# Merging three gated branches: the additions of the second and third branch as accumulating DMA transfers

## The chip, the cores and the metric

The kernel runs on one core of one Trainium2 chip. The metric is the device time in microseconds (us) of one execution; three executions of the kernel before were timed. The profile is one more execution, recorded by the hardware profiler; its times are counted from the start of its span, which runs from the first to the last instruction.

## What is computed

One layer of a decoder trunk on 256 tokens of width 2048, in float32. A normalised input goes through one wide projection; three mixers (a linear attention "GLA", a sparse attention "NSA" and a state-space mixer "SSD") each give an output of width 1024. Each is projected to 2048, multiplied by a sigmoid gate, and the three are added. The merged sum goes through an output projection, and a feed-forward network follows.

```python
gate = jax.nn.sigmoid(m_g).reshape(bsz, T, N_BRANCH, D)
merged = (gate[:, :, 0] * (y_gla @ w_branch[l, 0])
          + gate[:, :, 1] * (y_nsa @ w_branch[l, 1])
          + gate[:, :, 2] * (y_ssm @ w_branch[l, 2]))
x = x + rms_norm(merged @ w_out[l], norm_post_mix[l])
h = rms_norm(x, norm_pre_ffn[l])
f = (jax.nn.silu(h @ w_ffn_gate[l]) * (h @ w_ffn_up[l])) @ w_ffn_down[l]
```

## The kernel before, in words

All large products are streamed. The weights come from HBM in chunks of 512 KB (tile `raw`, four buffers), loaded by DMAs on the queue of SyncE (SP, line 75). Each chunk is split into two parts that the matrix engine multiplies at reduced precision: ScalarE (ACT) makes the high part `hi` (line 84), VectorE (DVE) the rest `lo` (line 87). There are three buffers of each. TensorE (PE) then multiplies a chunk in twelve matmuls of 128x512 (line 78): two blocks of 128 rows, two tiles of 128 tokens (t = 0 and t = 1), three products each. The activations are stationary; one product of 256 tokens by 512 features is `gemm_a`. In the last chunk of a `gemm_a` the token tiles go one after the other, so that t = 0 is ready earlier than t = 1.

The merge is `branch(b, ...)`. It is called for the SSD mixer first (it starts the sum), then for GLA, then for NSA (the last). In each call four groups of 512 features (j = 0 to 3) are worked on. For each j, a `gemm_a` of the input projection gives the gate, which ScalarE turns into `sg` by a sigmoid; then a `gemm_a` with `w_branch` gives the branch's product in PSUM, tile `g`. For each token tile, `ev` multiplies `sg` by `g` on VectorE (line 952); in the first branch the result is the sum `mg[j]` itself, in the other two it is written over `sg` and added to `mg[j]` by a second VectorE instruction (line 954). `mg[j]` of each token tile has 128 partitions of 512 floats, 256 KB.

In the last branch, when t = 1 is done, `to_fl` transposes the finished `mg[j]` on TensorE with eight small matmuls (tile `tr`, line 81), and ScalarE and VectorE split the result into `mh` and `ml`, the stationary operands of the output projection. The first of the two token tiles needs two of the eight transposes before the others, as the scheduler has placed them.

`sg` and `mg`, like most activations, sit in 32 buffers of one pool (`slot`), which are used again when their last reader is done. Work of the mixers that is not yet finished is woven in between the chunks: during the GLA branch it is the second half of the NSA mixer; during the last branch nothing is woven in. A scheduler places all instructions on the engines' queues ahead of time by its own cost estimates; each engine then takes its queue strictly in order. GpSimd (POOL) does a few set-up instructions at the start and one addition at the very end (line 1087).

Of the kernel before, what the change touches and what calls it, by code (L numbers as in the profile page):

```python
# [12 lines left out]
ALU = mybir.AluOpType  # L13
# [17 lines left out]
def trunk_kernel(ctx: ExitStack, tc: tile.TileContext, x, w_in, gla_a2, gla_a_bias, gla_norm,  # L31
# [36 lines left out]
    pinned = [False]  # L68

    def pin(ins):  # L70
        """In the pinned parts the engines keep the order in which the work is written down."""
        return tc.keep_in_program_order(ins) if pinned[0] else ins

    def dma(out, in_):
# [28 lines left out]
            kw["accum_out"] = acc  # L103
        return pin(S.activation(out=o, in_=a, func=f, scale=scale, **kw))  # L104

# [1 line left out]
    ident = const([P, P], name="ident")  # L107
    make_identity(nc, ident)
    eps = const([P, 1], name="eps")
# [1 line left out]
    one1 = const([P, 1], name="one1")  # L111
    V.memset(one1, 1.0)

    # parameters along the features, as columns
    cols, pcol = {}, {}

    def load_cols(key, parts):
# [50 lines left out]
        tt(lo, src, hi.bitcast(F32), ALU.subtract)  # L168

    def to_fl(src, hi, lo, i, gain=None):  # L170
        """Two feature tiles of src(k, t) = [tokens of tile t, features of tile k], transposed, scaled by
        their gains and split into hi and lo, as tiles 2i and 2i + 1 of the slot."""
        pt = pm("tr")
        for k in range(2):
            for t in range(2):
                tr(pt[:, k * T + t * P:k * T + (t + 1) * P], src(2 * i + k, t), ident)
        if gain is None:
            split(pt.rearrange("p (a n) -> p a n", a=2), hi[:, 2 * i:2 * i + 2, :], lo[:, 2 * i:2 * i + 2, :])
        else:
            for k in range(2):  # L180
                act(hi[:, 2 * i + k, :], pt[:, k * T:(k + 1) * T], AF.Copy, scale=gain(2 * i + k))
            for k in range(2):
                stt(lo[:, 2 * i + k, :], pt[:, k * T:(k + 1) * T], gain(2 * i + k), hi[:, 2 * i + k, :].bitcast(F32),
                    ALU.mult, ALU.subtract)
# [2 lines left out]
        act(o, a, AF.Sqrt, bias=eps[:, :], scale=1.0 / w)  # L187
        V.reciprocal(out=o, in_=o)

# [1 line left out]
    bg, started, first, raws = [], [], [], []  # L191

    def pump(n):
# [20 lines left out]
        while bg and (gen is None or any(b[0] is gen for b in bg)):  # L214
            pump(1)

# [1 line left out]
    def wchunk(fill, c, width):  # L218
        """The split goes ahead of the woven work; the loads too, once the activations are in."""
        if not started:  # L220
            return first.pop(0) if first else wchunk_(fill, c, width)
        with tc.high_priority(W_AHEAD):
            return wchunk_(fill, c, width)
# [19 lines left out]
        return fill  # L243

    def gemm_b(fill, width, xh, xl, KT, evac):
        """out[features, tokens]: the weights are stationary."""
        nt = width // P
        kc = 1024 // width
        g = [ps.tile([P, 2, T], F32, tag="g", bufs=4, name=nm("g")) for _ in range((nt + 1) // 2)]
        for c in range(KT // kc):  # L250
            hi, lo = wchunk(fill, c, width)
            for a in range(kc):
                k = c * kc + a
                for n in range(nt):
                    wh = hi[:, a * width + n * P:a * width + (n + 1) * P]
                    wl = lo[:, a * width + n * P:a * width + (n + 1) * P]
                    mm(g[n // 2][:, n % 2, :], wh, xh(k), k == 0 and n % 2 == 0, False)
                    mm(g[n // 2][:, n % 2, :], wh, xl(k), False, False)
                    mm(g[n // 2][:, n % 2, :], wl, xh(k), False, k == KT - 1)
            if c == KT // kc - 1:  # L260
                evac(g)
            tick()

    def gemm_a(fill, xh, xl, KT, evac, first=1, last=1):
        """out[tokens, 512 features]: the activations are stationary. The first and the last chunks go one
        token tile after the other, so that the tiles' beginnings and ends lie apart."""
        g = [ps.tile([P, 512], F32, tag="g", bufs=4, name=nm("g")) for _ in range(2)]
        n = KT // 2
        groups = [list(range(first))] + [[c] for c in range(first, n - last)] + [list(range(n - last, n))]
        for cs in groups:  # L270
            ws = [wchunk(fill, c, 512) for c in cs]
            ks = [(2 * c + a, hi[:, a * 512:(a + 1) * 512], lo[:, a * 512:(a + 1) * 512])
                  for c, (hi, lo) in zip(cs, ws) for a in range(2)]
            for t in range(2):
                for k, wh, wl in ks:
                    mm(g[t], xh(k)[:, t * P:(t + 1) * P], wh, k == 0, False)
                    mm(g[t], xh(k)[:, t * P:(t + 1) * P], wl, False, False)
                    mm(g[t], xl(k)[:, t * P:(t + 1) * P], wh, False, k == KT - 1)
                if cs[-1] == n - 1:
                    evac(g[t], t)  # L280
            for _ in cs:
                tick()

# [1 line left out]
    xt, hh, hl = [], [], []  # L285
    rsT = const([P, 2], name="rsT")
    rB = const([P, T], name="rB")
# [8 lines left out]
    first_fill = filler(w_in[0], C_SX, 512)  # L296

    def load_first():
        """The activations and the weights they meet first, the very first in small pieces."""
        pinned[0] = True  # L300
        for j in range(4):
            xt.append(slot(name="x"))
# [55 lines left out]
    def in_a(c0, evac):  # L358
        gemm_a(filler(w_in[0], c0, 512), hT, lT, 16, evac)

# [1 line left out]
    load_first()  # L362
    later(first_norm(), [1, 1, 1, 0, 1, 2, 2])
    conv = []
# [17 lines left out]
    for j in range(4):  # L382
        in_b(C_SX + 512 * j, 512, conv_evac(j))

# [1 line left out]
    sm = const([P, T], name="sm")  # L386

    def small_fill(c, raw):
# [6 lines left out]

    gemm_b(small_fill, 128, hT, lT, 16, lambda g: tt(sm, g[0][:, 0, :], rB, ALU.mult))

# [1 line left out]
    mneg = const([P, P], name="mneg")  # L399
    G.memset(mneg, 0.0)  # L400
    G.affine_select(out=mneg, in_=mneg, pattern=[[1, P]], compare_op=ALU.is_ge, fill=-1e30, base=0,
# [106 lines left out]
            ys_l.append(lo)  # L508

    def both(f):  # L510
        """An evacuation of both token tiles at the second one's end, for one table load."""
        gs = []

        def e(g, t):
            gs.append(g)
            if t == 1:
                f(gs[0], 0)
                pinned[0] = True
                f(gs[1], 1)
                pinned[0] = False  # L520
                gs.clear()
        return e
# [5 lines left out]
            act(halves(o[-1])[:, t, :], g, AF.Silu, scale=rsT[:, t:t + 1])  # L528
        return both(f)

# [1 line left out]
    eb, ei = [], []  # L532
    ebc = const([P, 8, 4], name="ebc")

    def decay():
        a2t = flat(slot(name="a2"))[:16, :]
        dma(out=a2t, in_=gla_a2[0])
        # one pass carries the products of the hi and lo parts, which lie one below the other
        a2s, sms = flat(slot(F32R, "a2s")), temp(F32R, "sms")[:, :T]
        for m, f in ((a2s, a2t), (sms, sm[:16, :])):  # L540
            V.memset(m[:96, :].bitcast(F32), 0.0)
# [134 lines left out]
            yg_h.append(hi)  # L676
            yg_l.append(lo)

# [1 line left out]
    nq, kv = [], []  # L680

    def nq_evac(g):
        """Queries, and for float32r: hi over lo of the even heads, lo over hi of the odd ones."""
        qf, L, QA, QB = slot(name="qf"), slot(F32R, "ql"), slot(F32R, "qa"), slot(F32R, "qb")
        for b in range(2):
            stt(qf[:, 2 * b:2 * b + 2, :], g[b], 0.125, rB2, ALU.mult, ALU.mult)
        for q_, H in ((slice(0, 64), QA), (slice(64, 128), QB)):
            S.copy(out=H[q_], in_=qf[q_])
            tt(L[q_], qf[q_], H[q_].bitcast(F32), ALU.subtract)
        dma(out=QA[64:128].bitcast(F32), in_=L[0:64].bitcast(F32))  # L690
        dma(out=QB[0:64].bitcast(F32), in_=L[64:128].bitcast(F32))
        nq.append((qf, QA, QB))
# [114 lines left out]
    def nsa(g):  # L807
# [30 lines left out]
                  pcm[:, 2:4, t * P:(t + 1) * P])  # L838
            yield

        # a pair of heads at a time; both full attentions and the compressed one add up in one accumulator,
        # the values' hi parts in its upper half and their lo parts in its lower half
        yt = slot(name="yn")
        hi, lo = slot(F32R, "ynh"), slot(F32R, "ynl")
        for f in range(4):
# [64 lines left out]
        yn_h.append(hi)  # L910
        yn_l.append(lo)

# [1 line left out]
    g_ssd, g_decay, g_gla, g_keys = ssd(), decay(), gla(), nsa_keys()  # L914
    finish()
    later(g_ssd, R_SSD)
# [17 lines left out]
    g_nsa = nsa(0)  # L934
    later(g_nsa, R_NSA)

# [1 line left out]
    mg = [None] * 4  # L938
    mh, ml = [], []

    def branch(b, yh, yl, first, last):
        for j in range(4):
# [5 lines left out]
            def ev(g, t):  # L948
                if first and t == 0:
                    mg[j] = slot(name="mg")  # L950
                sgt, mgt = halves(sg)[:, t, :], halves(mg[j])[:, t, :]
                tt(mgt if first else sgt, sgt, g, ALU.mult)
                if not first:
                    tt(mgt, mgt, sgt, ALU.add)
                if last and t == 1:
                    mh.append(slot(F32R, "mh"))
                    ml.append(slot(F32R, "ml"))
                    for i in range(2):
                        to_fl(lambda k, t: halves(mg[j])[:, t, k * P:(k + 1) * P], mh[j], ml[j], i)
# [11 lines left out]
    finish(g_nsa)  # L971
    branch(1, yn_h, yn_l, False, True)

# [1 line left out]
    gB = [slot(name="gB") for _ in range(2)]  # L975
    for h in range(2):
        dma(out=flat(gB[h]), in_=norm_post_mix[0, h * 1024:(h + 1) * 1024].partition_broadcast(P))
# [66 lines left out]
        for t in range(2):  # L1044
            token_rs(rs2, xss, t)

# [1 line left out]
    g_n2 = second_norm()  # L1048
    later(g_n2, 1.0)
    fh, fl = [], []  # L1050
# [67 lines left out]
```

## Time and profile before

| | |
|---|---|
| time, median of three executions | 1746.62 us (1746.36 to 1747.38) |
| span of the profiled execution | 1744.4 us (what lies around the span, against the median: 2.2 us) |
| TensorE busy | 1726.8 us, 99% of the span |
| VectorE busy | 1018.4 us, 58% |
| ScalarE busy | 857.3 us, 49% |
| GpSimd busy | 5.5 us |
| DMA, one hardware queue | 322.82 MB, 62.5% of 16 engines' span |
| the GLA and the NSA branch | about 622 to 778 us, and 778 to 916 us |

Only the span stands in the profile; the time of the profiled execution as a whole is not recorded, so the median of the three timed ones stands for it. A matmul's recorded duration overlaps the next one's (they are pipelined); the distance between their starts tells the rate. In the rows, PEld is the load of a stationary operand, which waits on behalf of the matmul that follows it. SPq is SyncE's own queue: a row there is the issue of a DMA, not its transfer.

### The profile page before, as it was taken

How to read it: one execution, taken by the hardware profiler on the slowest of the kernel's cores; microseconds unless marked ns; L12 is line 12 of the kernel's file. 1: busy time of each engine (PE TensorE's matmuls, PEld its weight loads, DVE VectorE, ACT ScalarE, POOL GpSimd, SP SyncE). 2: the span in 40 equal slices, each digit the busy share in tenths (PEclk: the TensorE clock that was granted, in tenths of full speed). 3: DMA queues.
4: the chain of work that ended last, by engine and by line, in shares of the span. 5: the costliest groups of instructions: out<-in, count | busy, mean ns of one | idle time of the engine just before them, and what ended most of it. 6: DMA issues, size and time to landing. Idle time of an engine off the chain costs nothing.

```text
span 1744.4 us, 22985 instructions
## 1 busy us (share of the span) xinstructions
PE 1726.8 (99%) x8951; PEld 1463.6 (84%) x8951; DVE 1018.4 (58%) x1366; ACT 857.3 (49%) x1129; POOL 5.5 (0%) x37
## 2 busy tenths in 40 slices
PE   8999999999999999999999999999999999999998
PEld 8998889999887887788888778888888888888886
DVE  5687667565766666765555564544544545544444
ACT  6556467343656556554444464444444444443443
POOL 0000000000000000000000000000000000000000
PEclk9999999999999999999999999999999999999999
DMA  7666655755555565556667676666666666766664
GB/s 234 183 175 194 178 170 171 215 146 156 171 157 159 167 182 157 157 158 191 190 185 251 194 221 189 192 184 190 191 185 190 190 186 191 225 205 195 205 205 147
DMA packets 178497, 324.28 MB, mean 186 GB/s; under 512 B 21010, under 2 KB 24772, under 8 KB 178388
## 3 DMA queue, kind: packets, MB, share of 16 engines
q1 hardware_dynamic: 178388, 322.82, 62.5%
q8 instruction: 70, 1.15, 0.3%
q14 instruction: 39, 0.32, 0.1%
HBM read 316.47 MB, written 4.21 MB: 184 GB/s over the span
## 4 chain that ended last, share of the span: by engine, by line
PE 96%; DVE 1%; ACT 1%; DMA 1%; issue 1%; SPq 0%; DVEq 0%; ACTq 0%
PE g L78 89%; PE tr L81 1%; PE po L78 1%; PE ps L78 1%; DMA raw<-in_w_in_dram 1%; DVE lo L87 1%; PE p L81 1%; PE py L78 1%; PE pa L78 1%; PE m L81 0%; ACT x L104 0%; ACT hi L84 0%; DVE ab L576 0%; PE ph L78 0%; DMA x<-in_x_dram 0%
## 5 line engine op out<-in xcount | busy, mean ns | idle before, releaser
L87 DVE TENSOR_TENSOR lo<-raw,hi 128x1024 fp32r<-128x1024 f32 (+1 forms) x583 | 712.3, 1222 | 654.7 <-ACT hi L84 653.5
L84 ACT CAST hi<-raw 128x1024 fp32r<-128x1024 f32 (+1 forms) x583 | 611.9, 1050 | 802.4 <-PE g L78 765.7
L78 PE MATMUL g<-lo,fh 128*128 128x512 f32 x1056 | 412.2, 390 | 1.4 <-DVE lo L87 1.4
L78 PE MATMUL g<-hi,fl 128*128 128x512 f32 x1056 | 412.1, 390 | 0.0
L78 PE MATMUL g<-hi,fh 128*128 128x512 f32 x1056 | 411.3, 390 | 0.0
L78 PEld LDWEIGHTS g<-lo,fh 128*128 128x128 f32 x1056 | 198.3, 188 | 42.7 <-DVE lo L87 1.9
L78 PEld LDWEIGHTS g<-hi,fl 128*128 128x128 f32 x1056 | 198.4, 188 | 40.7 <-DVE fl L96 0.4
L78 PEld LDWEIGHTS g<-hi,fh 128*128 128x128 f32 x1056 | 198.3, 188 | 40.7 <-ACT fh L104 0.2
L78 PE MATMUL g<-hi,hh 128*128 128x512 f32 x576 | 229.9, 399 | 0.0
L78 PE MATMUL g<-lo,hh 128*128 128x512 f32 x576 | 226.1, 392 | 0.0
L78 PE MATMUL g<-hi,hl 128*128 128x512 f32 x576 | 225.8, 392 | 0.0
L78 PE MATMUL g<-hh,hi 128*128 128x256 f32 x752 | 215.6, 287 | 0.0
L78 PE MATMUL g<-hh,lo 128*128 128x256 f32 x752 | 213.6, 285 | 1.5 <-DVE lo L87 1.5
L78 PE MATMUL g<-hl,hi 128*128 128x256 f32 x752 | 213.2, 284 | 0.0
L78 PEld LDWEIGHTS g<-hh,lo 128*128 128x128 f32 x752 | 144.5, 192 | 2.6 <-DVE lo L87 2.5
L78 PEld LDWEIGHTS g<-hh,hi 128*128 128x128 f32 x752 | 144.8, 193 | 0.4
L78 PEld LDWEIGHTS g<-hl,hi 128*128 128x128 f32 x752 | 144.9, 193 | 0.1
L78 PEld LDWEIGHTS g<-hi,hh 128*128 128x128 f32 x576 | 108.4, 188 | 23.2 <-ACT hi L84 0.7
L78 PEld LDWEIGHTS g<-hi,hl 128*128 128x128 f32 x576 | 108.2, 188 | 22.5
L78 PEld LDWEIGHTS g<-lo,hh 128*128 128x128 f32 x576 | 108.4, 188 | 20.3
L104 ACT ACT_TABLE_LOAD x43 | 55.2, 1283 | 4.0 <-DVE ab L576 2.5
L78 PE MATMUL g<-hi,ml 128*128 128x512 f32 x128 | 50.1, 391 | 0.0
(275 smaller groups left out, 1337.6 us busy)
## 6 DMA issues: line engine op xcount, KB each, us to landing
raw<-in_w_in_dram SPq DMA_DIRECT2D x235, 512.0 KB, 3.6
raw<-in_w_ffn_gate_dram SPq DMA_DIRECT2D x88, 512.0 KB, 3.7
raw<-in_w_ffn_up_dram SPq DMA_DIRECT2D x88, 512.0 KB, 3.7
raw<-in_w_ffn_down_dram SPq DMA_DIRECT2D x88, 512.0 KB, 4.6
raw<-in_w_branch_dram SPq DMA_DIRECT2D x48, 512.0 KB, 3.8
raw<-in_w_out_dram SPq DMA_DIRECT2D x32, 512.0 KB, 4.3
x<-in_x_dram SPq DMA_DIRECT2D x7, 512.0 KB, 6.0
cumB<-scr SPq DMA_DIRECT2D x4, 512.0 KB, 5.5
```

Of the source, the lines that this page charges most:

```text
L78: PE.matmul(o, lhsT=l, rhs=r, start=start, stop=stop, skip_group_check=True)
L81: pin(PE.transpose(o, a, i))
L84: pin(S.copy(out=o, in_=a))
L87: pin(V.tensor_tensor(out=o, in0=a, in1=b, op=op))
L104: return pin(S.activation(out=o, in_=a, func=f, scale=scale, **kw))
```

## The change

Line 954 is replaced. The product of the second and third branch is still made on VectorE; the addition to `mg[j]` is a DMA, issued from GpSimd's queue, that reads `sg` and accumulates it onto `mg[j]`, both in SBUF. There are 16 such DMAs of 256 KB: two branches, four groups, two token tiles. The rest of the text's difference is comments and docstrings that were taken out.

```diff
                 sgt, mgt = halves(sg)[:, t, :], halves(mg[j])[:, t, :]
                 tt(mgt if first else sgt, sgt, g, ALU.mult)
                 if not first:
-                    tt(mgt, mgt, sgt, ALU.add)
+                    G.dma_start(out=mgt, in_=sgt, accum_op=ALU.add)
                 if last and t == 1:
```

On TensorE, at the end of the last branch's last group (j = 3). `mg_5935` is the merged sum of this group, `tr_8470` and `tr_8477` the PSUM tiles of its transposes; `g_8496` and `g_8497` are the two token tiles of the next product (the output projection's first), whose first chunk is `hi_8500`, `lo_8501` and the second `hi_8518`, `lo_8519`. Of the kernel before, from the seventh matmul of that first chunk on:

```order
L78 MATMUL g_8497<-hi_8500,mh_7739 128x512
L78 MATMUL g_8497<-lo_8501,mh_7739 128x512
L81 MATMUL tr_8470<-ident_72,mg_5935 128x128 [waits DVE_49,PE_49]
L81 MATMUL tr_8477<-ident_72,mg_5935 128x128 [waits PE_49]
L78 MATMUL g_8497<-hi_8500,ml_7740 128x512
L78 MATMUL g_8497<-hi_8500,mh_7739 128x512
L78 MATMUL g_8497<-lo_8501,mh_7739 128x512
L78 MATMUL g_8497<-hi_8500,ml_7740 128x512
L78 MATMUL g_8496<-hi_8518,mh_7739 128x512 [waits Activation_49]
L78 MATMUL g_8496<-lo_8519,mh_7739 128x512
L81 MATMUL tr_8470<-ident_72,mg_5935 128x128 [waits DVE_49]
L81 MATMUL tr_8470<-ident_72,mg_5935 128x128 x2
```

Of the changed kernel, from the last matmul of the first chunk on:

```order
L78 MATMUL g_8497<-hi_8500,ml_7740 128x512
L78 MATMUL g_8496<-hi_8518,mh_7739 128x512 [waits Activation_49]
L78 MATMUL g_8496<-lo_8519,mh_7739 128x512 [waits DVE_49]
L81 MATMUL tr_8470<-ident_72,mg_5935 128x128 [waits DMASW6_49,PE_49]
L81 MATMUL tr_8477<-ident_72,mg_5935 128x128 [waits PE_49]
L78 MATMUL g_8496<-hi_8518,ml_7740 128x512
L78 MATMUL g_8496<-hi_8518,mh_7739 128x512
L81 MATMUL tr_8470<-ident_72,mg_5935 128x128 [waits DMASW7_49]
L81 MATMUL tr_8470<-ident_72,mg_5935 128x128 x2
L81 MATMUL tr_8477<-ident_72,mg_5935 128x128 x3
L78 MATMUL g_8496<-lo_8519,mh_7739 128x512
```

The transposes of t = 0 stood behind eight matmuls of the next product and waited for VectorE; now they stand behind fourteen and wait for a DMA from GpSimd (DMASW6). Those of t = 1 stood behind fourteen matmuls and stand behind sixteen (DMASW7). The other three groups of the last branch read the same.

On GpSimd's queue, the last rows of the program, of the changed kernel (of these, the kernel before has the one of line 1087):

```order
L954 DMA mg_5613<-sg_7998 128x512 [waits DMASW4_49,DVE_49]
L954 DMA mg_5613<-sg_7998 128x512 [waits DMASW5_49,DVE_49]
L954 DMA mg_5935<-sg_8241 128x512 [waits DMASW6_49,DVE_49]
L954 DMA mg_5935<-sg_8241 128x512 [waits DMASW7_49,DVE_49]
L1087 TENSOR_TENSOR x_2154_12694<-no_13901,x_2154_12694 128x512 [waits DMAHW0_49,PE_49,Activation_49]
```

Each DMA waits for its product on VectorE and for the same group's DMA of the branch before; nothing else stands between them on this queue.

On SyncE's queue, a little later: `x_1373` is the input for the residual, loaded into the buffer that `sg_8241` leaves. Before:

```order
L75 DMA raw_8652<-in_w_out_dram 128x2x512 [waits DMAHW5_49,DVE_49]
L75 DMA raw_8670<-in_w_out_dram 128x2x512 [waits DMAHW6_49,DVE_49]
L75 DMA x_1373_8488<-in_x_dram 128x2x512
L75 DMA raw_8688<-in_w_out_dram 128x2x512 [waits DMAHW7_49,DVE_49]
L75 DMA raw_8706<-in_w_out_dram 128x2x512 [waits DMAHW1_49,DVE_49]
```

After:

```order
L75 DMA raw_8652<-in_w_out_dram 128x2x512 [waits DMAHW5_49,DVE_49]
L75 DMA x_1373_8488<-in_x_dram 128x2x512 [waits DMASW7_49,DMASW6_49]
L75 DMA raw_8670<-in_w_out_dram 128x2x512 [waits DMAHW6_49,DVE_49]
L75 DMA raw_8688<-in_w_out_dram 128x2x512 [waits DMAHW7_49,DVE_49]
L75 DMA raw_8706<-in_w_out_dram 128x2x512 [waits DMAHW1_49,DVE_49]
```

The load of `x_1373` moved ahead of one weight load and waits for the last two accumulations.

In the first two groups of the GLA branch the scheduler also moved the woven NSA work: VectorE's scalings of `sw` come earlier by the additions that are gone, and the transposes of `sw` on TensorE some ten matmuls earlier.

## Rows read from the trace of the kernel before

**Rows 1.** The page: busy time by engine, and the chain that ended last

```profile
PE 1726.8 (99%) x8951; PEld 1463.6 (84%) x8951; DVE 1018.4 (58%) x1366; ACT 857.3 (49%) x1129; POOL 5.5 (0%) x37
...
PE 96%; DVE 1%; ACT 1%; DMA 1%; issue 1%; SPq 0%; DVEq 0%; ACTq 0%
```

**Rows 2.** Stretches: busy us (instructions) by engine, granted clock, DMA share, GB/s

```profile
650.00:800.00 150.00, 149.99 (x679) 119.22 (x678) 100.30 (x156) 85.15 (x142) 0.00 (x0) 1.00 0.55 161
800.00:920.00 120.00, 120.00 (x546) 98.96 (x545) 66.16 (x67) 55.01 (x60) 0.00 (x0) 1.00 0.65 192
911.00:918.00 7.00, 7.00 (x36) 5.72 (x35) 6.08 (x9) 4.22 (x5) 0.00 (x0) 1.00 0.70 211
```

**Rows 3.** Waits from 800 to 930 us: us in total, times, longest

```profile
ACT hi L84 <- PE g L78: 70.5, 46, 1.9
DVE lo L87 <- ACT hi L84: 58.6, 42, 1.5
...
PEld tr L81 <- DVE mg L87: 0.9, 4, 0.2
```

**Rows 4.** Tile mg: its additions, ns min/median/max, first and last start

```profile
L87 DVE TENSOR_TENSOR mg<-mg,sg x16: 639/684/692, 657.9 to 914.3; 128x512 f32<-128x512 f32 x16
```

**Rows 5.** Waits of PEld from 640 to 800 us (most of it the GLA branch)

```profile
PEld ps L78 <- issue: 5.3, 20, 0.4
...
PEld po L78 <- ACT w L84: 0.5, 2, 0.3
...
PEld p L81 <- DVE sw L91: 0.4, 2, 0.2
```

**Rows 6.** Timeline, end of the last group: start, us, engine, line, instruction

```profile
911.36 1.28 DVE L87 TENSOR_TENSOR sg<-sg,g 128x512 f32<-128x512 f32 x2
...
911.47 3.30 SPq L75 DMA_DIRECT2D raw<-in_w_out_dram  x2
911.65 0.39 PE L78 MATMUL g<-hi,mh 128*128 128x512 f32 x1
...
912.56 0.68 DVE L87 TENSOR_TENSOR mg<-mg,sg 128x512 f32<-128x512 f32 x1
...
913.16 1.22 DVE L87 TENSOR_TENSOR lo<-raw,hi 128x1024 fp32r<-128x1024 f32 x1
```

**Rows 7.** The chain from 800 to 920 us: start, us, piece

```profile
882.30 31.33 PE g L78 x138
913.63 0.22 PE tr L81 x2
```

**Rows 8.** DMA issues: engine, count, KB each, median us to landing

```profile
raw<-in_w_out_dram SPq DMA_DIRECT2D x32, 512.0 KB, 4.3
...
x1d<-x SPq DMA_DIRECT2D x4, 512.0 KB, 6.1
...
out_dram<-x SPq DMA_DIRECT2D x8, 256.0 KB, 2.4
...
qa<-ql SPq DMA_DIRECT2D x2, 256.0 KB, 4.3
```

**Rows 9.** Timeline of SyncE's queue about 440 us and about 920 us

```profile
439.59 0.37 SPq L75 DMA_DIRECT2D raw<-in_w_in_dram  x1
440.79 0.47 SPq L75 DMA_DIRECT2D qa<-ql  x1
...
920.59 3.08 SPq L75 DMA_DIRECT2D raw<-in_w_out_dram  x2
923.72 0.47 SPq L75 DMA_DIRECT2D x<-in_x_dram  x1
```

## The prediction

> **What bounds the kernel now.** I read the page first: TensorE is busy for 99% of the span and makes up 96% of the chain that ended last [rows 1]. So a microsecond of another engine is worth something only where TensorE waits for it. The stretches that hold the two changed branches say the same more sharply: TensorE is busy for 149.99 of 150 us and for all of 120 us, at the full granted clock (1.00, the 2.4 GHz level), while VectorE works 100 of 150 and 66 of 120 us [rows 2]. The waits give the direction: ScalarE's splits wait for TensorE (70.5 us), VectorE's for ScalarE (58.6 us) [rows 3]; weights are there early and everyone waits for the matmuls. What the sum's additions cost TensorE today is one row: four waits of the transposes for `mg`, 0.9 us in all, all in the last branch [rows 3].
>
> **What is removed.** 16 additions of 0.684 us on VectorE, 10.9 us of its 1018 [rows 1, 4]. Almost none of that is on the path. In the last branch it is at most the 0.9 us of waits. In the GLA branch nobody waits for `mg`, but the woven NSA work shares VectorE; the waits there that VectorE's or ScalarE's being late could explain are 0.4 and 0.5 us, in two pieces each, while the largest row of TensorE's waits has no engine behind it [rows 5]. The reordered `sw` work in two groups arrives earlier on both engines by about the same amount; I put it at 0, with 1 us either way over both groups (about the sum of those two rows).
>
> **What is added, and where it lies.** In the GLA branch the eight transfers have no reader until the same group of the next branch, more than 100 us later; they cost nothing on the path. In the last branch TensorE itself stands before the transposes, and everything behind them on its queue waits too. So the price is set at four places, one per group, and the question is one time: from the end of a product on VectorE to the landing of its transfer.
>
> How much of it is covered, at j = 3. The two products run on VectorE from 911.36 to 912.64, 0.68 us each with a small overlap; so t = 0 ends at about 912.04 and t = 1 at 912.64 [rows 6]. The next product's first matmul starts at 911.65 [rows 6]. Matmuls follow at 31.33/138 = 0.227 us [rows 7]. The transposes of t = 0 now stand behind fourteen of them: 911.65 + 14 x 0.227 = 914.83. Then two transposes (0.22 [rows 7]) and two matmuls (0.45): 915.50 for t = 1. So both transfers have about 2.8 us (914.83 - 912.04 = 2.79, 915.50 - 912.64 = 2.86) before TensorE stops.
>
> How long a transfer takes. No transfer of the kernel before is issued by GpSimd, and none accumulates, so this is a bound from both sides. The lower end is 2.4 us: 256 KB from SBUF to HBM at the end of the kernel, with no weights beside it [rows 8]. The nearest row is `qa<-ql`: 256 KB within SBUF, issued 1.2 us behind a weight load as the accumulation will be 0.6 to 1.2 us behind one (911.47): 4.3 us [rows 6, 8, 9]. An accumulation moves more than a copy, since it reads the sum as well as the product; twice the bytes beside weight loads is `x1d<-x`, 512 KB, 6.1 us [rows 8]. I take the middle of 4.3 and 6.1, **5.2 us**. The descriptors, which GpSimd makes, the second transfer behind the first, and an addition that must read before it writes have no row; a whole further round trip for them (2.4 us) on top of 6.1 gives the upper end, 8.5 us.
>
> The wait at one place: 912.04 + 5.2 - 914.83 = 2.4 us for t = 0; t = 1 then lands at 917.84, and TensorE gets to it at 915.50 + 2.4 = 917.9, with no further wait. Four places: 9.6 us. None of it comes back: TensorE has no idle time later in which to catch up, and the work that piles up meanwhile (splits of the next weights) was waiting for TensorE already [rows 3].
>
> What else is queued behind these waits. ScalarE's and VectorE's splits of the transposes (`mh`, `ml`) come later, with the split of a weight chunk behind them on each queue; TensorE has one chunk under way and two more split by then, about 2 x 12 x 0.227 = 5.4 us of work, which covers a split (1.22 us on VectorE [rows 6]). `mh` of the last group is needed in the seventh chunk of the output projection, six chunks or 16 us on. On SyncE, the load of `x_1373` now waits for the last transfers, with a weight load behind it. It is reached after `raw_8652`, at 920.59 + 0.37 = 920.96 [rows 9], 8.3 us after the last product, so a transfer of 5.2 us has landed; and the weight load behind it was not free to go before some 923.3 (it and the one before fill 920.59 to 923.67 [rows 9]). Cost nothing; it would begin to cost past some 10 us.
>
> **The sum.** Against the profiled execution, 1744.4 us of span: 4 x 2.4 = +9.6, the waits for VectorE's addition -0.9, the woven work 0: 1753.1 us. The median of the timed runs is 2.2 us above this span: **1755.3 us**, 0.5% slower.
>
> **The rivals.** *The transfer is hidden.* It lands in at most 2.8 us, TensorE never waits, and 0.9 us of waits go: 1744.4 - 0.9 + 2.2 = 1745.7 us. For it speaks the 2.4 us row [rows 8], against it that this row has the DMA engines to itself, while here weight loads take 0.70 of them [rows 2]. It decides at the landing: with up to 3.95 us (a wait of 1.16 at each place, 4.6 - 0.9 = 3.7 us in all) the time stays within 0.2% of before, so this is the case that ends not slower. The Trainium skill speaks for it: "DMA: Bandwidth & Descriptors", section on the anatomy of one DMA on the GpSimd path, has a fit of about 2.0 us plus the bytes at 436 GB/s, by which an estimate for 256 KB is 2.6 us and the sum would be 1745.7 us; no run here shows a transfer on that path yet, and the row for 256 KB within SBUF is 4.3 us from another queue.
>
> *GpSimd is held up by VectorE.* Straight behind the second product VectorE runs a split of 1.22 us, `lo<-raw,hi` [rows 6] (it moves up to about 912.6, since the addition is gone). If GpSimd could not make descriptors while VectorE works in SBUF, each transfer would start up to 1.2 us later: 4 x (2.4 + 1.2) - 0.9 = +13.5, 1760 us. Nothing in the trace bears on it, as GpSimd is idle there [rows 2].
>
> *VectorE's relief is worth more than its waits.* For a gain of over 3.5 us the transfers would have to be hidden and the woven work of the GLA branch speed up by over 2.6 us; its waits on VectorE and ScalarE are below 1 us [rows 5].
>
> **How the numbers follow.** The forecast, landings between 3.95 and 8.5 us: 0.68. Held up by VectorE: 0.08. Hidden or nearly: 0.22. The gain: 0.02. Differences within 0.2% (3.5 us) are about what a measurement of this kernel can tell from no change; so faster 0.02, same 0.22, slower 0.68 + 0.08 = 0.76. The ends of the unknown: hidden, with 1 us of luck, 1744.7; the upper end, 912.04 + 8.5 - 914.83 = 5.7 us at four places, 22.8 - 0.9 + 1 = +22.9, 1769.5 us. For 8 in 10 I cut a part at either end: 1747 to 1767.
>
> **What would show it.** Right: TensorE's weight loads for `tr` wait about 2.4 us for the DMA `mg<-sg` at four places (t = 0), near 814, 850, 886 and 922 us, and hardly at t = 1; the transfers land 5.2 us after issue; VectorE's busy time falls by 11 us; SyncE's `x` load waits for none. Wrong: landings under 3 us with no such wait (hidden), landings that follow VectorE's splits (held up), a wait at t = 1 as long as at t = 0 (the two transfers go one after the other), or a change outside the four places: in the woven part from 650 to 800 us, or in the weight loads' landing.

## The result, and the profile after

The changed kernel takes 1765.58 us (median of four runs, 1765.24 to 1768.27) against 1746.86 us for the kernel before (four runs): the ratio is 1.011, 95% interval 1.0097 to 1.0122. It is slower, by 18.7 us where 8.7 was forecast. The profiled execution has a span of 1764.1 us, 19.7 more than before. It is one of the four; TensorE's granted clock, averaged over the span, was 0.994 to 0.996 in them (0.995 in the profiled one), so how much of the work ran at the lower clock differs a little from one to the next.

The page of the changed kernel, busy time and the chain that ended last, answering [rows 1]:

```profile
span 1764.1 us, 23020 instructions
...
PE 1733.7 (98%) x8951; PEld 1468.0 (83%) x8951; DVE 1010.3 (57%) x1350; ACT 858.7 (49%) x1129; POOL 19.6 (1%) x53
...
PE 88%; issue 7%; DMA 2%; DVE 2%; ACT 1%; POOL 0%; SPq 0%; DVEq 0%; POOLq 0%; ACTq 0%
```

VectorE has its sixteen instructions less and GpSimd its sixteen more. TensorE, with the same 8951 matmuls, is busy for 6.9 us longer, and it also stands for longer: 19.7 - 6.9 leaves 12.8 us of new idle time. So there are two losses, and the forecast had only one kind.

The idle time is in the waits from 640 to 960 us of the changed kernel, which holds both branches (engine and line, what it waited for: us in total, times, longest). It answers the last row of [rows 3], where these transposes waited 0.9 us for VectorE:

```profile
PE tr L81 <- DMA mg<-sg: 11.6, 8, 1.9
PEld tr L81 <- issue: 8.3, 4, 2.3
...
PEld tr L81 <- DMA mg<-sg: 6.7, 4, 1.7
```

TensorE waited for the transfers eight times, at all four groups of the last branch, once for each token tile; the PEld rows are the same stops seen by the load of the stationary operand. The waits of the woven work in the GLA branch [rows 5] stand as they were (its largest row is 5.3 us before and after).

The first of the four places, in the timeline of the changed kernel (start, us, engine, line, instruction; in brackets the idle time before it and what ended it), answering [rows 6]:

```profile
810.96 1.28 DVE L87 TENSOR_TENSOR sg<-sg,g 128x512 f32<-128x512 f32 x2
...
811.94 1.75 POOL L954 DMA_DIRECT2D mg<-sg  x2 [31.77 <-DVE sg L87]
...
814.20 0.39 PE L78 MATMUL g<-lo,hh 128*128 128x512 f32 x1
...
816.25 0.41 PE L81 MATMUL tr<-ident,mg 128*128 128x128 f32 x2 [1.66 <-DMA mg<-sg]
...
816.73 0.40 PE L78 MATMUL g<-hi,hh 128*128 128x512 f32 x1
818.38 1.19 PE L81 MATMUL tr<-ident,mg 128*128 128x128 f32 x6 [1.26 <-DMA mg<-sg]
...
819.80 0.63 PE L78 MATMUL g<-hi,hl 128*128 128x512 f32 x1
...
820.23 0.63 PE L78 MATMUL g<-hi,hh 128*128 128x512 f32 x1
```

The first product ends at about 811.64 and its transfer has landed by 816.2, 4.6 us later; the second ends at 812.24 and its transfer has landed by 818.35, 6.1 us later. TensorE stops for 1.66 us, does two transposes and two matmuls, and stops for another 1.26 us. Then the matmuls, 0.39 us long and 0.227 apart until then, are 0.63 us long and 0.43 apart. The stretches of the changed kernel around it, and two later ones (columns as in [rows 2]), say why:

```profile
811.00:814.40 3.40, 3.40 (x16) 2.63 (x14) 2.47 (x4) 1.28 (x2) 1.75 (x2) 1.00 0.75 210
814.40:818.40 4.00, 1.08 (x6) 0.49 (x5) 1.23 (x1) 0.82 (x1) 0.00 (x0) 1.00 1.05 202
818.40:822.40 4.00, 4.00 (x14) 3.37 (x15) 1.33 (x2) 1.18 (x2) 0.00 (x0) 0.57 0.45 173
822.40:826.00 3.60, 3.60 (x18) 2.98 (x17) 1.23 (x1) 1.61 (x2) 0.00 (x0) 1.00 0.00 0
895.00:899.00 4.00, 4.00 (x21) 3.41 (x22) 1.52 (x3) 2.13 (x3) 0.00 (x0) 1.00 0.47 177
932.60:936.60 4.00, 4.00 (x17) 3.39 (x16) 1.33 (x2) 3.16 (x5) 0.00 (x0) 0.72 0.93 338
1024.00:1027.00 3.00, 3.00 (x14) 2.48 (x13) 2.55 (x8) 1.95 (x8) 0.00 (x0) 0.50 0.92 270
```

TensorE is busy for only 1.08 of the 4 us in which it stops twice, at a granted clock of 1.00, and behind the stops the clock is 0.57 over 4 us: most of it is granted at the lower level, 1.2 GHz. At 822.4 it is back at 2.4 GHz; in finer slices the lower level lasts from about 818.7 to 822.2, 3.5 us. The same is seen behind the second and the fourth place (3.1 and 3.5 us), not behind the third (895 to 899: 1.00), and once more in the norm that follows the output projection (1024 to 1027: 0.50), where the kernel before has 1.00 for the same work.

The norm's lower clock is not shown to come from the change. One of the kernels below has the merge of the kernel before and only adds three transfers behind the end of the program; its norm has the lower clock too (the first row is of the kernel before, the second of that kernel):

```profile
1006.00:1009.00 3.00, 3.00 (x21) 2.39 (x19) 3.00 (x8) 2.95 (x11) 0.00 (x0) 1.00 1.02 337
...
1006.60:1009.60 3.00, 3.00 (x13) 2.35 (x12) 2.79 (x8) 2.17 (x9) 0.00 (x0) 0.50 0.96 331
```

**Where the 19.7 us are.** Each place begins with a pair of `sg<-sg,g` products, and the norm begins with a transpose of `x`. Their starts in the kernel before (the last place is in [rows 6]):

```profile
810.56 1.28 DVE L87 TENSOR_TENSOR sg<-sg,g 128x512 f32<-128x512 f32 x2
...
844.15 1.28 DVE L87 TENSOR_TENSOR sg<-sg,g 128x512 f32<-128x512 f32 x2
...
877.75 1.28 DVE L87 TENSOR_TENSOR sg<-sg,g 128x512 f32<-128x512 f32 x2
...
998.19 0.63 PE L81 MATMUL m<-ident,x 128*128 128x128 f32 x4
```

And in the changed kernel, behind the first at 810.96:

```profile
849.44 1.28 DVE L87 TENSOR_TENSOR sg<-sg,g 128x512 f32<-128x512 f32 x2
...
887.66 1.28 DVE L87 TENSOR_TENSOR sg<-sg,g 128x512 f32<-128x512 f32 x2
...
924.40 1.28 DVE L87 TENSOR_TENSOR sg<-sg,g 128x512 f32<-128x512 f32 x2
...
1016.07 0.63 PE L81 MATMUL m<-ident,x 128*128 128x128 f32 x4
```

From one to the next took 33.59, 33.60, 33.61 and 86.83 us, and takes 38.48, 38.22, 36.74 and 91.67: the four places cost 4.9, 4.6, 3.1 and 4.8 us, 17.5 in all. The rest is 0.4 us ahead of the first place, and 1.8 us from the norm to the end (746.21 us before, 748.03 after). Of these 1.8 us 1.4 go with the norm's clock: from the norm's first transpose to GpSimd's addition at line 1087 it is 740.56 us before, 741.92 in the changed kernel, and 741.88 in the kernel with the unchanged merge. The 0.4 us mean nothing either, since that kernel reaches the first place 0.55 us later than the kernel before. The third place, with the clock at 1.00 throughout, gives the price of the stops and of getting going again behind them, 3.1 us; so an estimate of 1.5 to 1.8 us of each other place, some 5 us of the 17.5, goes with the lower clock (4.4 us if the differences between the places' stops, 2.8 to 3.1 us, are taken off).

### The profile page after: what moved, and what is told of

The parts are those of the page before. It is cut to its first block, busy times and chain, and to the rows that moved or that the text cites. A ratio compares the mean times of both kernels' runs of the same rounds, so it can differ in the third digit from the quotient of the medians.

```text
span 1764.1 us, 23020 instructions
## 1 busy us (share of the span) xinstructions
PE 1733.7 (98%) x8951; PEld 1468.0 (83%) x8951; DVE 1010.3 (57%) x1350; ACT 858.7 (49%) x1129; POOL 19.6 (1%) x53
## 3 DMA queue, kind: packets, MB, share of 16 engines
q8 instruction: 70, 1.15, 0.3%
## 4 chain that ended last, share of the span: by engine, by line
PE 88%; issue 7%; DMA 2%; DVE 2%; ACT 1%; POOL 0%; SPq 0%; DVEq 0%; POOLq 0%; ACTq 0%
PE g L78 82%; PE tr L81 1%; PE po L78 1%; PE ps L78 1%; DMA raw<-in_w_in_dram 1%; DVE lo L87 1%; DMA mg<-sg 1%; PE p L81 1%; PE py L78 1%; PE pa L78 1%; ACT hi L84 0%; POOL mg L954 0%; PE m L81 0%; SPq L75 0%; ACT x L104 0%
## 5 line engine op out<-in xcount | busy, mean ns | idle before, releaser
L78 PE MATMUL g<-lo,mh 128*128 128x512 f32 x128 | 50.3, 393 | 0.0
```

What stands on the lines that cost most here:

```text
L78: PE.matmul(o, lhsT=l, rhs=r, start=start, stop=stop, skip_group_check=True)
```

## The experiments

My theory after this first look: the whole loss is made in the last branch; the landing is late because an accumulating transfer is slow and the second shares the way with the first, and a stop of about 3 us is followed by the lower clock. Rivals: the GLA branch takes part; GpSimd is held up by VectorE; only the place of the transposes in TensorE's queue is at fault. Below, what a place costs is the distance between the pairs of `sg<-sg,g` (and to the norm) less that of the kernel before, as above.

**Which branch.** The accumulating transfers in the GLA branch alone, and in the last branch alone:

```diff
-                    G.dma_start(out=mgt, in_=sgt, accum_op=ALU.add)
+                    if last:
+                        tt(mgt, mgt, sgt, ALU.add)
+                    else:
+                        G.dma_start(out=mgt, in_=sgt, accum_op=ALU.add)
```

> Only the second (GLA) branch adds by accumulating DMA; the last branch adds on VectorE as before. Theory: the eight transfers of this branch have no reader for over 100 us, so the whole loss (18.7 us) comes from the last branch; this kernel takes the time of before, 1746.9 us within 2 us, and TensorE's matmuls keep the full clock. Rival (the loss is spread over both branches, through slower weight loads or the reordered woven work): 1750 us or more.

For the second kernel the condition is `if not last`:

> Only the last branch adds by accumulating DMA. Theory: all of the loss is at its four places, waits of about 1.8 us for t = 0 and 1.3 us for t = 1 and a stretch at half the granted clock behind most of them: 1764 to 1768 us, like the changed kernel. Rival (spread over both branches): 1755 to 1760 us.

The GLA branch alone takes 1747.32 us, ratio 1.0005 (0.9996 to 1.0015), though its eight transfers need 3.6 to 6.4 us to land. The last branch alone takes 1767.78 us, 1.0123 (1.0106 to 1.014). So the whole loss is in the last branch. Its four places cost 4.7, 3.2, 4.7 and 3.8 us, and its lower clock lies behind the first and the third: which places have it differs between two programs that do the same there. The longest stops of all, 1.72 and 1.63 us at the fourth place here, kept the full clock. As a profile is one execution (this one took 1765.05 us, the other three 1767.33 to 1768.66), it may well differ between two executions of one kernel too; that is not shown.

**The transfer without the addition.** These two kernels copy `sg` over `mg` instead of adding it; one from GpSimd's queue, one from SyncE's.

```diff
-                    G.dma_start(out=mgt, in_=sgt, accum_op=ALU.add)
+                    G.dma_start(out=mgt, in_=sgt)
```

> The 16 transfers are issued from GpSimd as plain copies onto the sum, without the addition, so the merged sum holds the last branch alone; places and order stay. If the accumulation (a second read, the addition) is what makes a transfer late, landings fall from a median of 5.3 to 3.5 to 4 us, the waits to under 1 us a place, and the time to 1747 to 1752 us. If it is GpSimd's queue (descriptors made one transfer after the other), landings stay at about 5 us and the time at 1760 to 1766 us.

```diff
-                    G.dma_start(out=mgt, in_=sgt, accum_op=ALU.add)
+                    nc.sync.dma_start(out=mgt, in_=sgt)
```

> The same 16 plain copies, without the addition, from SyncE's hardware queue; the scheduler puts the transposes behind 17 and 20 matmuls instead of 14 and 16, so the cover is about 3.5 us for t = 0 and 3.8 us for t = 1. With the 4.3 us of the copy within SBUF in the kernel before, TensorE waits under 1 us a place: 1747 to 1752 us. Rival (any transfer of 256 KB beside the weight loads lands after 5 us or later): 1755 us or more, like the changed kernel.

Tile `mg` in the kernel that copies from GpSimd (duration of the issue, min/median/max in ns; then the landing):

```profile
L954 POOL DMA_DIRECT2D mg<-sg x16: 546/546/706, 658.3 to 917.5; - x16
...
DMA to landing us min/median/max: 2.3/3.5/5.4
```

And in the changed kernel:

```profile
L954 POOL DMA_DIRECT2D mg<-sg x16: 853/867/1199, 657.8 to 926.0; - x16
...
DMA to landing us min/median/max: 3.5/5.3/6.5
```

Without the addition the same 16 transfers are issued in 0.55 instead of 0.87 us and land after 3.5 instead of 5.3 us. The time is 1753.68 us, 1.0038 (1.0023 to 1.0053); the places cost 1.1, 1.6, 0.9 and 2.9 us, with the clock at 1.00 behind each. From SyncE it is 1750.63 us, 1.002 (1.001 to 1.003), landings 3.9 us in the median, places 0.6, 0.5, 0.6 and 1.2, clock 1.00 behind them (but the lower level for some 3.3 us in the norm); there the scheduler puts the transposes a little later, behind 17 and 20 matmuls, so the two do not compare the queues alone. A plain copy would still not be free at this point of the program, but some 12 of the 18.7 us go with its being an accumulation.

**One transfer at a place.** In the last branch, a transfer for t = 0 alone, or for t = 1 alone, and VectorE's addition otherwise:

```diff
-                    G.dma_start(out=mgt, in_=sgt, accum_op=ALU.add)
+                    if not last or t == 1:      # the other kernel: t == 0
+                        tt(mgt, mgt, sgt, ALU.add)
+                    else:
+                        G.dma_start(out=mgt, in_=sgt, accum_op=ALU.add)
```

> In the last branch only t = 0 is added by DMA, t = 1 and the whole GLA branch on VectorE; all eight transposes stand behind 14 matmuls. Theory: one transfer alone at a place lands as t = 0 does in the changed kernel, so TensorE waits about 1.8 us at each of four places and no second time: +7 us if the clock holds, 1753 us; if TensorE's clock halves behind even such a wait, up to 1760 us. Rival (the second transfer's cost is a cost of two transfers sharing the engines, so that one alone is faster): waits under 1 us, 1747 to 1750 us.

> In the last branch only t = 1 is added by DMA. Its transposes stand behind 16 matmuls as in the changed kernel, those of t = 0 behind 8 as before. Theory: without t = 0's transfer ahead of it, t = 1's lands about 4.6 us after its product instead of 6.1, TensorE waits about 1.7 us at four places: 1753 us if the clock holds. Rival (t = 1 is late because of its place among the weight loads, not because of t = 0's transfer): a landing of 6 us after the product, waits of 3.2 us a place, 1759 us or more.

1755.79 us, 1.0048 (1.0033 to 1.0063), and 1755.28 us, 1.0046 (1.003 to 1.0063). The single transfers land 4.1 and 3.6 us after their issue (medians). Places cost 1.8 to 2.6 and 1.2 to 1.6 us, with the clock at 1.00. In the changed kernel the same two take 4.2 and 5.8 us at the first place: the one that goes first is hardly slower in company, the second is by 2 us.

**One transfer of both halves.** One accumulation of 512 KB per group, when t = 1 is done:

```diff
-                    G.dma_start(out=mgt, in_=sgt, accum_op=ALU.add)
+                    if t == 1:
+                        G.dma_start(out=flat(mg[j]), in_=flat(sg), accum_op=ALU.add)
```

> One accumulating DMA of 512 KB for both token tiles, issued after t = 1's product; the eight transposes stand behind 20 matmuls (cover 3.6 us). If the engines' time for the bytes sets the landing, it comes at 6 us after the product or later: a wait of 2.5 us or more a place, 1757 to 1766 us. If the fixed part sets it, it lands like one of 256 KB, at about 4.6 us: a wait of 1 us, 1750 to 1752 us.

1762.91 us, 1.0091 (1.0076 to 1.0106). It is issued in 0.86 us, as long as one of 256 KB, and lands after 5.4 to 7.5 us (5.8 in the median); the transposes stand behind 20 matmuls. There is one stop at each place, in its timeline:

```profile
818.78 1.06 PE L81 MATMUL tr<-ident,mg 128*128 128x128 f32 x8 [2.49 <-DMA mg<-sg]
...
854.96 1.94 PE L81 MATMUL tr<-ident,mg 128*128 128x128 f32 x8 [2.41 <-DMA mg<-sg]
...
892.49 1.94 PE L81 MATMUL tr<-ident,mg 128*128 128x128 f32 x8 [2.37 <-DMA mg<-sg]
...
930.22 1.94 PE L81 MATMUL tr<-ident,mg 128*128 128x128 f32 x8 [2.51 <-DMA mg<-sg]
```

Four stops within 0.14 us of each other in length; behind the first the eight transposes take 1.06 us, behind the others 1.94: the lower clock again, and the places cost 2.7, 4.0, 4.0 and 4.0 us. It is worth about 1.3 us a place here. And the length of the stop is not what decides: the longest but one kept the clock.

**The accumulation alone.** To the kernel before, three chained transfers of 256 KB within SBUF are added behind its last store: an accumulation from GpSimd, a copy from GpSimd, a copy from SyncE.

```diff
             dma(out=out[0, t * P:(t + 1) * P, 512 * j:512 * (j + 1)], in_=xo)
+        if t == 1:
+            xs, fs_ = [halves(x2[j])[:, 1, :] for j in range(4)], [halves(fo[j])[:, 1, :] for j in range(4)]
+            G.dma_start(out=xs[3], in_=fs_[3], accum_op=ALU.add)
+            G.dma_start(out=fs_[1], in_=xs[3])
+            nc.sync.dma_start(out=xs[2], in_=fs_[1])
```

> The kernel before, with three transfers of 256 KB within SBUF behind the last store, one after the other, with nothing beside them: an accumulating one from GpSimd, a plain one from GpSimd, a plain one from SyncE. The output is already stored. It prices each alone. If weight loads beside it make the accumulation late in the merge, it lands within 3.5 us here; if not, after 4.2 us or more. A plain copy from GpSimd: 2.6 to 3.2 us; from SyncE 2.2 us. The time grows by their sum, 7 to 10 us.

The DMA view of this kernel from 1742 to 1756 us, in 40 slices of 0.35 us (busy tenths of the DMA engines, GB/s; then the issues):

```profile
DMA  9935999400000000999900000495000069300000
GB/s 375 386 141 193 380 392 374 158 0 0 0 0 0 0 0 0 181 193 193 181 0 0 0 0 0 176 374 199 0 0 0 0 228 392 129 0 0 0 0 0
...
x<-no POOLq DMA_DIRECT2D x1, 256.0 KB, 3.5
no<-x POOLq DMA_DIRECT2D x1, 256.0 KB, 2.4
```

With every engine idle and no weights under way, the accumulation lands after 3.5 us, the copy after 2.4. The accumulation (the run of four slices) keeps the DMA engines busy for 1.4 us at 181 to 193 GB/s; the copies behind it (three slices each, the outer ones only in part) reach 374 and 392. Half the rate is what the Trainium skill would lead one to expect: "Collectives: The Full Stack", section on the bandwidth ceiling, says of a ReduceScatter that its add needs two source reads, and that it so runs at half the rate of an AllGather, which copies; the trace agrees in the ratio, with 181 to 193 against 374 to 392 GB/s. Its issue takes 1.04 us here, against 0.87 us in the median beside VectorE's work; so there is no sign that VectorE holds GpSimd up. And 3.5 us is more than the 2.8 us of cover at a place: even an undisturbed transfer would have been late.

**The transposes later.** The change as it is, with the transposes three weight chunks further on (behind 36 matmuls of the next product), and two chunks (24):

```diff
+    def late(j):
+        for i in range(2):
+            to_fl(lambda k, t: halves(mg[j])[:, t, k * P:(k + 1) * P], mh[j], ml[j], i)
+        yield
...
-                    for i in range(2):
-                        to_fl(lambda k, t: halves(mg[j])[:, t, k * P:(k + 1) * P], mh[j], ml[j], i)
+                    later(late(j), [0, 0, 0, 1])        # two chunks: [0, 0, 1]
```

> All 16 accumulations by DMA; the transposes of a finished group are written three chunks later, and stand behind 36 matmuls: a cover of 7.9 us for t = 0 and 7.3 us for t = 1. Theory (too little cover is the whole cause): no wait, no stretch at half the clock, 1746 to 1748 us, the time of before. Rival (the transfers cost something in themselves, by slowing weight loads or the engines): 1750 us or more with the waits gone.

> As with three chunks of delay, but two: the transposes stand behind 24 matmuls, a cover of about 5.1 us for t = 0 and 4.6 us for t = 1. Theory: t = 0 lands in time (4.6 us), t = 1 (6.1 us) does not; one wait of about 1.5 us a place, 1752 us if the clock holds behind a single short wait. Rival (the landing shifts with the transposes, since TensorE's progress sets the weight loads beside it): no wait or one over 2 us.

And the kernel before, with VectorE's additions, with the same three chunks:

> The kernel before with its additions on VectorE and the transposes three chunks later. The four waits for VectorE's addition (0.9 us in all) go: 1746 us, the same as before within what can be measured. It shows what the delay of the transposes does by itself. Rival (the delay costs something, as splits pile up): 1750 us.

Three chunks: 1746.85 us, 0.9999 (0.9989 to 1.0008). The transfers are as slow as ever, the landings of tile `mg` there read

```profile
DMA to landing us min/median/max: 3.3/5.3/6.6
```

but no transpose waits for one and no place costs anything (-0.03 us each). Two chunks: 1754.65 us, 1.0045 (1.0032 to 1.0059); places 1.9, 1.5, 1.6 and 1.9 us, the clock at 1.00. The kernel before with three chunks: 1746.53 us, 0.9998 (0.9989 to 1.0007). So the loss at the places is the late landing and what follows from it. The lower clock is part of that: with the same transfers, as slow, but no stop, the granted clock is 1.00 from 800 to 1000 us, so the transfers beside TensorE's work do not lower it by themselves. Twelve matmuls decide between a loss of some 8 us and none; and once the landing is covered, sixteen additions off VectorE give nothing back that these runs can tell. No version of these beats the kernel before.

**The stop filled.** Between the two landings of a place, two useless float32 matmuls (four instructions in the rows), so that TensorE works where it stopped the second time:

```diff
+                    pf = pm("fill")
+                    for i in range(2):
+                        mm(pf[:, :512], ident, halves(mg[j])[:, 0, :512], True, True)
                     for i in range(2):
                         to_fl(lambda k, t: halves(mg[j])[:, t, k * P:(k + 1) * P], mh[j], ml[j], i)
```

> The changed kernel with two useless float32 matmuls of 128x512 (the identity by the merged sum of t = 0; nobody reads the result) at each of the four places, behind the landing of t = 0 and ahead of the transposes; two of the product's matmuls move behind. So TensorE still has to wait for both landings, but works for most of the time between the first and the second, instead of stopping twice. Theory (the half clock at a place follows from the length of the stop): the granted clock stays at 1.00 at all four places; a place costs what the later landing costs at the full clock, 3.1 us (third place of the changed kernel), and 0.45 us for the two matmuls that moved behind it: 4 x 3.6 = 14.4 us, with 0.4 us at the start and 0.5 at the end as in the changed kernel 15 us, about 1762 us. Rival (the half clock comes from something else at these places, such as the transfers' work in SBUF or the late landing itself): half clock as in the changed kernel at three of four places, 1765.6 + 4 x 0.45 = about 1767 us.

1764.24 us, 1.0098 (1.0081 to 1.0115): neither expectation. Its timeline at the first three places:

```profile
816.69 3.65 PE L78 MATMUL fill<-mg,ident 128*128 128x512 f32 x4 [1.96 <-DMA mg<-sg]
...
855.58 1.96 PE L78 MATMUL fill<-mg,ident 128*128 128x512 f32 x4 [1.67 <-DMA mg<-sg]
...
892.84 1.96 PE L78 MATMUL fill<-mg,ident 128*128 128x512 f32 x4 [1.48 <-DMA mg<-sg]
```

The fills run at the full clock at three places (1.96 us; the fourth like these) and at the lower level at the first (3.65 us), behind a single stop of 1.96 us. The places cost 5.6, 3.9, 3.6 and 4.5 us, and from the norm to the end the kernel takes only 0.2 us more than before, at the full clock. So one place of four had the lower clock instead of three. That would fit a link with the second stop, but does not show one: the kernel with the last branch alone had the lower clock at two places with nothing filled. The filling gained nothing at the places, 17.5 us in all as before, since the fills outlast the second landing at three of them and the two matmuls of the product come behind it; the 1.3 us against the changed kernel lie in the norm. And the first place fell behind one stop of 1.96 us, while the kernel with a transfer for t = 0 alone held the clock behind stops of 1.7 to 2.4 us. What picks the place is left open.

## Why the prediction was right or wrong, point by point

*Direction, place and kind of loss: right.* TensorE waits for `mg<-sg` at the four places named, everything else in the last branch had time to spare, and moving the transposes out of the landing's reach takes the whole loss away.

*What is removed: right.* VectorE's relief is worth nothing measurable. Its busy time fell by 8.1 us, not by 10.9. Part of the difference is that neighbouring instructions overlap in the records (the addition at 912.56 ends at 913.24, the split behind it starts at 913.16 [rows 6]); the rest is not explained.

*GLA branch and SyncE: right.* The GLA branch alone is within 0.05%; the load of `x` waited for no transfer.

*The landing of t = 0: near.* Chosen was 5.2 us after the product, measured 4.6; the wait of 2.4 us was 1.66 in the row of the first place.

*The landing of t = 1: the step that failed first.* The prediction gave both transfers the same 5.2 us, so that the wait for t = 0 covered t = 1. Measured are 6.1 us after the product and a second stop of 1.26 us: "with no further wait" is wrong, and the prediction's own sign of it (a wait at t = 1 as long as at t = 0) nearly came. Tile `mg` at the first place of the changed kernel (issues, ns min/median/max and starts; then the landings from the issue's start):

```profile
L954 POOL DMA_DIRECT2D mg<-sg x2: 853/1000/1148, 811.9 to 812.5; - x2
...
DMA to landing us min/median/max: 4.2/5.0/5.8
```

Each issue starts 0.3 us after its product, but the second takes 1.15 us instead of 0.85, since the first is not done; that is 0.3 of the 1.5 us between the two. The rest fits the DMA engines, which an accumulation needs for about 1.4 us even by itself; that t = 1 alone lands after 3.6 us instead of 5.8 shows that the first transfer is the cause, but not whether it is by the engines' time or by order in the queue. The queues' shares of the 16 engines from 811.9 to 818.5 us of the changed kernel (packets, MB):

```profile
q0 software_dynamic: 288, 0.52, 54.9%
q1 hardware_dynamic: 465, 0.91, 44.3%
```

GpSimd's queue takes 55% of the engines' time with 0.52 MB, the weight loads 44% with 0.91: by this count the engines have nothing left in these 6.6 us. The prediction had named "the second transfer behind the first" among the things without a row, and put it into the upper end only; it belonged in the sum. A place without the lower clock costs 3.1 us (the third; its two stops are 2.8 us of it) instead of 2.2 (the wait of 2.4 less 0.2 for the one that was there), four of them 12.5 us instead of 8.7.

*The term that was missing, and the larger of the two: the clock.* The sum took TensorE's rate from the kernel before, where the granted clock is 1.00 through these stretches [rows 2], and put what follows a wait at nothing. Behind three of the four places TensorE was granted the 1.2 GHz level for 3.1 to 3.5 us; that is about 5.0 us (17.5 less 12.5). With 0.4 us ahead of the first place and 1.8 us from the norm on this is the whole difference: 0.4 + 12.5 + 5.0 + 1.8 = 19.7 us of span, against 8.7. What is shown: the lower clock at the places came with late landings (four kernels with places at 2.7 us and more had it behind some of them; the five whose places cost 0.5 to 2.9 us had 1.00 behind all). What decides at one place is not. Nor are the 1.8 us shown to come from the change: the norm had the lower clock in the changed kernel, in the one with the last branch alone, in the one that copies from SyncE, whose stops were short, and in the one with the unchanged merge, which has no such stops; it had the full clock in the kernel with one transfer of 512 KB, whose stops were long.

*"None of it comes back": right,* and it was too mild, as work behind a stop ran slower.

*The rivals.* Hidden: wrong here; it becomes true with 22 more matmuls of cover. The fit in "DMA: Bandwidth & Descriptors" that spoke for it (an estimate of 2.6 us by the Trainium skill) agrees with the lone copy (2.4 us), not with the accumulation (3.5 alone, 5.3 beside weight loads). GpSimd held up by VectorE: its time, 1760 us, was nearer than the forecast, but for another reason, as the issue is no shorter with VectorE idle.

*The range* held the time (1747 to 1767), close to its upper end, and that is luck in part. The upper end had been widened for the second transfer and the read before the write, and these are late, but a landing of 6.1 us for t = 1 gives by the prediction's own sum 912.64 + 6.1 - 915.50 = 3.2 us a place and 1759 us; the rest came from the clock, which the range did not have.

## What to carry to other kernels

Before an addition is taken off an engine that has time, look at what waits for its result: an addition of 0.68 us with its reader 2 us behind became a transfer of 4 to 6 us, and that is free only where the reader stands further off (here behind 36 matmuls of 0.227 us instead of 14). Cost the last of several transfers that start together, not the first, with the issue time of each and, for accumulations, the DMA engines' time at half a copy's rate. And where TensorE, busy without a gap so far, gets a stop of 2 to 3 us, leave room in the range for a lower clock behind it (here 1.3 to 1.8 us a place, at some places and not at others).

## What the runs showed of the hardware

- An accumulating transfer of 256 KB within SBUF, alone on the chip, takes 3.5 us and moves 181 to 193 GB/s; a plain one from GpSimd 2.4 us, at up to 374. Beside weight loads the two have medians of 5.3 and 3.5 us.
- GpSimd needs 0.87 us to issue an accumulation and 0.55 us to issue a copy, of 256 KB, and 0.86 us for an accumulation of 512 KB, so it did not grow between these two sizes.
- One 512 KB accumulation landed in 5.8 us in the median, about as late as the second of two of 256 KB (5.5 to 6.0 us at the four places of the changed kernel).
- Behind stops of 2.0 to 3.1 us at a place TensorE was granted the 1.2 GHz level for 3.1 to 3.5 us in some places, and none of it in others that look alike (four stops of 2.37 to 2.51 us in one kernel: the first without, three with; two stops of 3.35 us together in another: without).
- The norm behind the merge had the lower clock in one kernel whose merge was left as it was, and the full clock in the kernel before: 1.3 us between two programs that do the same up to their last store.
